# Latent attention in steps of one block of queries, with the projections and the heads' scales cut into pieces between the steps

## The chip, the core and the metric

One core of one Trainium2 chip runs the whole program. The metric is the device time of one execution in microseconds (us). Below, PE is the matrix engine (TensorE), DVE the vector engine (VectorE), ACT the scalar engine (ScalarE), POOL is GpSimd and SP issues the loads. Each engine takes its instructions in one fixed order, which the build of the program sets, and waits at an instruction until what it needs is there.

## What is computed

A trunk of two layers over 512 tokens of width 1,024, in float32. The first layer mixes by a state-space scan and gated linear attention, the second by latent attention with 16 heads; a SwiGLU network follows each. The change is in the latent attention alone:

```python
cq, ckv, k_rope = jnp.split(h @ w_dqkv, [384, 384 + 256], axis=-1)
q = (rms_norm(cq, q_lora_norm) @ w_uq).reshape(bsz, seqlen, H, 64 + 32)
kv = (rms_norm(ckv, kv_lora_norm) @ w_ukv).reshape(bsz, seqlen, H, 64 + 64)
...
q_nope = rms_norm(q_nope, q_nope_norm)
q_rope = apply_rope(rms_norm(q_rope, q_rope_norm), cos[:, None, :], sin[:, None, :])
k_nope = rms_norm(k_nope, k_nope_norm)
...
p = jax.nn.softmax(jnp.where(mask, s, -jnp.inf), axis=-1).astype(v.dtype)
return jnp.einsum('bhqk,bkhv->bqhv', p, v)   # blocks of 128 queries, causal
...
return o @ w_o
```

So each head's queries are scaled twice (64 plain and 32 rotated numbers) and its keys once, by factors that are known only when all of a head's numbers for a token are there.

## The kernel before, in words

Dense products run in three passes of split float32 (`mm3`, L159 to L163): a weight is loaded on SP (`wraw`), split by ACT into `whi` (L155) and by DVE into `wlo` (L156), and multiplied into one of three PSUM accumulators (`acc`, `NACC = 3`), which ACT or DVE empties. There are two more PSUM buffers for scores (`sco`), two for transposes of probabilities (`ptr`), and one for the values' product (`po`).

The attention layer begins with the low-rank products for queries (`q`, three columns) and keys and values (`kv`, two), each followed by the tokens' factors: eight tiny products with ones (L847), then on DVE the mean squares `lm` (L849 to L851), a Newton iteration (`rsqrt`, L176 to L181, tiles `lri`, `lry`, `lrt`) and a last product (L853) into `cf`.

`project(g)` makes one of four groups of four heads: four blocks of queries `qs` (products of 384 columns, emptied by ACT at L911 with the factor of `q`), four blocks of keys and values (512 columns, emptied at L924 and L925 with the factor of `kv`), and then the heads' scales: squares on ACT (L929, L932), their sums on DVE (L930, L931, L933), `rsqrt` over all three kinds at once (`hri`, `hry`, `hrt`), and the scaling and rotation of the whole group (L938 to L945, with `rope` at L863 to L866).

`prepare` transposes the keys (L952) and queries (L965) of a pair of heads on PE and copies them to `kT` (L959 on ACT, L961 on DVE) and `qT` (L967 on ACT). `attend` does a pair: for each of four blocks of queries, the scores of both heads (L984), the negative row minimum on DVE with the mask (L987), the exponential on ACT (L989), the reciprocal (L992) and the scaling (L995) on DVE, transposes on PE (L998), copies to `pt` on ACT (L1002); then the values' product for all blocks (L1007) and its split into `xh`, `xl`. `o_round` is the output projection of four pairs, added to `X` at L1026.

The calls at the end set the order: both first groups are projected, then the pairs follow each other, with the next pair's `prepare` before each `attend`, `project(2)` and `project(3)` behind pairs 0 and 2, and `o_round(0)` behind pair 4. A scheduler of the build moves instructions forward from there by priority, weights by 90 places, so that dense products of a later call fill in between a pair's steps.

```python
pr = {0: project(0), 1: project(1)}
ready = prepare(0, 0, *pr[0])
for p in range(8):
    g, hp = divmod(p, 2)
    cur = ready
    if p < 7:
        ready = prepare((p + 1) // 2, (p + 1) % 2, *pr[(p + 1) // 2])
    attend(g, hp, pr[g][2], *cur)
    if p in PROJ:
        pr[2 + PROJ.index(p)] = project(2 + PROJ.index(p))
    if p == 4:
        o_round(0)
```

Of the kernel before, what the change touches and what calls it, by code (L numbers as in the profile page):

```python
# [18 lines left out]
P = 128  # L19
# [13 lines left out]
PROJ = (0, 2)  # L33
# [16 lines left out]
def kernel(ctx: ExitStack, tc: tile.TileContext, A, yT, stop=99):  # L50
# [120 lines left out]
    def rsqrt(pool, m, shape, tag, ytag=""):  # L171
# [3 lines left out]
        t = pool.tile(shape, F32, tag=tag + "t", name=nm(tag + "t"), bufs=1)  # L175
        V.tensor_scalar(h, m.bitcast(I32), 1, None, ALU.logical_shift_right)  # L176
# [609 lines left out]
    with tc.tile_pool(name="mla", bufs=2) as mp, tc.tile_pool(name="mla1", bufs=1) as m1:  # L786
# [40 lines left out]
        lora, cf = {}, {}  # L827
        for who, n0, n in (("q", 0, 3), ("kv", 3, 2)):
            lora[who], ssq = [], None
            for c in range(n):  # L830
                w = weight(A["w_dqkv"][n0 + c], KD, P)
                ps = acc()
                dense(ps, w, xp)
                hi = m1.tile([P, T], F32R, name=nm("lh"))
                lo = m1.tile([P, T], F32R, name=nm("ll"))
                g = col(who + "_lora", c)
                S.activation(hi, ps, AF.Copy, scale=g)
                V.scalar_tensor_tensor(lo, ps, g, hi.bitcast(F32), ALU.mult, ALU.subtract)
                lora[who].append((hi, lo))
                sq = res.tile([P, T], F32, tag="sq", name=nm("lsq"), bufs=2)  # L840
                S.activation(sq, ps, AF.Square)
                if ssq is not None:
                    V.tensor_tensor(sq, sq, ssq, ALU.add)
                ssq = sq
            ps = aux()
            for i in range(4):
                E.matmul(ps[:, i:i + 1], ssq[:, i * P:(i + 1) * P], ones[:, 0:1], start=True, stop=True)  # L847
# [6 lines left out]
            cf[who] = f  # L854

# [43 lines left out]
        def project(g):  # L899


            qs = mp.tile([P, 4, 4, 96], F32, tag="qs", name=nm("qs"))
            wqs = [weight(A["w_uq"][g, :, k0:k0 + n], n, 384) for k0, n in ((0, 2), (2, 1))]
            for i in range(4):
                ps = acc()
                for k in range(3):
# [4 lines left out]
                S.activation(qs[:, i].rearrange("p h d -> p (h d)"), ps[:, :384], AF.Copy,  # L911
                             scale=cf["q"][:, i:i + 1])
# [3 lines left out]
            v = mp.tile([P, 4, 4, 64], F32, tag="v", name=nm("v"), bufs=3)  # L916
            for i in range(4):
# [16 lines left out]
            for j, n in enumerate((64, 32, 64)):  # L934
                V.tensor_scalar(st[:, j], st[:, j], 1.0 / n, EPS, ALU.mult, ALU.add)
# [81 lines left out]
        def o_round(r, nxt=None):  # L1017

            for m2 in range(4):
                w = weight(A["w_o"][r, m2], 4, 256)  # L1020
                for j in range(2):
# [5 lines left out]
                    if nxt is not None:  # L1027
                        nxt.add(m)
# [102 lines left out]
```

## Time and profile before

| what | value |
|---|---|
| device time, median of 3 runs | 1362.85 us (1362.34 to 1363.99) |
| the profiled execution | 1362.29 us, of which the span from first to last instruction is 1360.1 us |
| busy in the span | PE 1341.3 us (99%), PE's weight loads 1088.2 us (80%), DVE 811.1 us (60%), ACT 567.5 us (42%) |
| TensorE's granted clock | 1.00 of full speed in all 40 slices |
| attention layer | from about 780 us to about 1,002 us of the span |

Products on PE are pipelined: a row's duration covers its way through the array, and the next one starts before it ends. What a product costs in a full stream is the distance from its start to the next start. Busy time therefore hides short waits, and the text below goes by starts. On DVE and ACT, too, an instruction that does not need the one before it starts some 0.07 to 0.1 us before that one's end.

### The profile page before, as it was taken

How to read it: one execution, taken by the hardware profiler on the slowest of the kernel's cores; microseconds unless marked ns; L12 is line 12 of the kernel's file. 1: busy time of each engine (PE TensorE's matmuls, PEld its weight loads, DVE VectorE, ACT ScalarE, POOL GpSimd, SP SyncE). 2: the span in 40 equal slices, each digit the busy share in tenths (PEclk: the TensorE clock that was granted, in tenths of full speed). 3: DMA queues.
4: the chain of work that ended last, by engine and by line, in shares of the span. 5: the costliest groups of instructions: out<-in, count | busy, mean ns of one | idle time of the engine just before them, and what ended most of it. 6: DMA issues, size and time to landing. Idle time of an engine off the chain costs nothing.

```text
span 1360.1 us, 16680 instructions
## 1 busy us (share of the span) xinstructions
PE 1341.3 (99%) x6506; PEld 1088.2 (80%) x6506; DVE 811.1 (60%) x1363; ACT 567.5 (42%) x946; POOL 7.8 (1%) x35
## 2 busy tenths in 40 slices
PE   9999999999999999999999999999999999999998
PEld 5798889888888888888888887657688888888887
DVE  7877977878876444444333569776584444443221
ACT  7575624644353322322222358775653223222121
POOL 0000000000000000000000000000000000000000
PEclk9999999999999999999999999999999999999999
DMA  5342232322232223323333321111033332233331
GB/s 178 123 142 79 78 109 70 95 71 63 90 97 93 93 94 103 98 93 93 98 101 97 102 67 55 32 47 62 4 106 93 94 104 97 93 96 106 112 103 64
DMA packets 36782, 122.23 MB, mean 90 GB/s; under 512 B 4768, under 2 KB 5792, under 8 KB 36704
## 3 DMA queue, kind: packets, MB, share of 16 engines
q1 hardware_dynamic: 35888, 120.72, 28.6%
q8 instruction: 51, 0.84, 0.2%
q10 hardware_dynamic: 816, 0.46, 0.1%
q14 instruction: 27, 0.22, 0.0%
HBM read 119.03 MB, written 2.13 MB: 89 GB/s over the span
## 4 chain that ended last, share of the span: by engine, by line
PE 89%; DVE 7%; ACT 3%; issue 1%; DMA 0%; SPq 0%; DVEq 0%; ACTq 0%
PE acc L161 27%; PE acc L162 27%; PE acc L163 26%; PE sco L984 2%; PE ptr L998 1%; PE po L1007 1%; DVE wlo L156 1%; PE a L496 1%; DVE cva L406 1%; PE a L693 1%; PE a L682 0%; PE a L480 0%; ACT whi L155 0%; PE a L500 0%; PE a L695 0%
## 5 line engine op out<-in xcount | busy, mean ns | idle before, releaser
L155 ACT CAST whi<-wraw 128x1024 fp32r<-128x1024 f32 (+2 forms) x221 | 225.7, 1022 | 548.1 <-PE acc L162 425.0
L161 PE MATMUL acc<-xh,whi 128*128 128x512 f32 x1144 | 449.5, 393 | 2.8 <-ACT qT L967 1.6
L162 PE MATMUL acc<-xl,whi 128*128 128x512 f32 x1144 | 447.5, 391 | 0.0
L163 PE MATMUL acc<-xh,wlo 128*128 128x512 f32 x1144 | 447.2, 391 | 0.0
L156 DVE TENSOR_TENSOR wlo<-wraw,whi 128x1024 fp32r<-128x1024 f32 (+2 forms) x221 | 261.8, 1185 | 159.0 <-ACT whi L155 158.7
L161 PEld LDWEIGHTS acc<-xh,whi 128*128 128x128 f32 x1144 | 214.7, 188 | 47.9 <-ACT qT L967 1.8
L163 PEld LDWEIGHTS acc<-xh,wlo 128*128 128x128 f32 x1144 | 214.8, 188 | 45.2 <-issue 0.7
L162 PEld LDWEIGHTS acc<-xl,whi 128*128 128x128 f32 x1144 | 214.9, 188 | 44.2 <-issue 1.0
L756 DVE TENSOR_TENSOR fu<-acc,R 128x512 f32<-128x512 f32 x44 | 30.4, 691 | 137.1 <-PE acc L163 137.1
L163 PE MATMUL acc<-fhh,wlo 128*128 128x512 f32 x288 | 112.0, 389 | 0.0
L161 PE MATMUL acc<-fhh,whi 128*128 128x512 f32 x288 | 112.0, 389 | 0.0
L162 PE MATMUL acc<-fhl,whi 128*128 128x512 f32 x288 | 112.0, 389 | 0.0
L753 DVE TENSOR_TENSOR fg<-acc,R 128x512 f32<-128x512 f32 x44 | 30.4, 691 | 88.7 <-PE acc L163 88.6
L162 PEld LDWEIGHTS acc<-fhl,whi 128*128 128x128 f32 x288 | 54.1, 188 | 11.3
L161 PEld LDWEIGHTS acc<-fhh,whi 128*128 128x128 f32 x288 | 54.1, 188 | 11.2
L163 PEld LDWEIGHTS acc<-fhh,wlo 128*128 128x128 f32 x288 | 54.1, 188 | 11.1
L162 PE MATMUL acc<-mxl,whi 128*128 128x512 f32 x128 | 50.0, 392 | 0.0
L161 PE MATMUL acc<-mxh,whi 128*128 128x512 f32 x128 | 49.7, 390 | 0.0
L163 PE MATMUL acc<-mxh,wlo 128*128 128x512 f32 x128 | 49.7, 390 | 0.0
L984 PE MATMUL sco<-kT,qT 96*128 96x128 f32 (+3 forms) x128 | 42.8, 445 | 1.5 <-DVE mx L987 1.3
L987 DVE CUSTOM_DVE_ANT_0 sc<-sco,am 128x128 f32<-128x128 f32 (+3 forms) x64 | 30.7, 487 | 13.6 <-PE sco L984 11.5
L989 ACT ACTIVATE sc<-sc,mx 128x128 f32<-128x128 f32 (+3 forms) x64 | 35.7, 561 | 7.3 <-DVE mx L987 7.0
(345 smaller groups left out, 1583.8 us busy)
## 6 DMA issues: line engine op xcount, KB each, us to landing
wraw<-in_w_gate_dram SPq DMA_DIRECT2D x44, 512.0 KB, 3.5
wraw<-in_w_up_dram SPq DMA_DIRECT2D x44, 512.0 KB, 3.5
wraw<-in_w_down_dram SPq DMA_DIRECT2D x32, 512.0 KB, 3.5
wraw<-in_w_out_dram SPq DMA_DIRECT2D x16, 512.0 KB, 3.5
wraw<-in_w_xbc_dram SPq DMA_DIRECT2D x12, 512.0 KB, 3.6
wraw<-in_w_down_dram SPq DMA_DIRECT2D x16, 384.0 KB, 3.1
wraw<-in_w_z_dram SPq DMA_DIRECT2D x8, 512.0 KB, 3.5
wraw<-in_w_v_dram SPq DMA_DIRECT2D x8, 512.0 KB, 3.5
```

Source lines behind the costliest of these rows:

```text
L155: S.copy(hi[:, :kc * m], r)
L156: V.tensor_tensor(lo[:, :kc * m], r, hi.bitcast(F32)[:, :kc * m], ALU.subtract)
L161: E.matmul(out, ah, bh, start=first, stop=False)
L162: E.matmul(out, ah, bl, start=False, stop=False)
L163: return E.matmul(out, al, bh, start=False, stop=last)
L406: V.scalar_tensor_tensor(a, xpad[:, k:k + T], cw[:, 12 * k + i:12 * k + i + 1], a, ALU.mult, ALU.add)
L496: E.matmul(pd[64 * h:64 * h + 64, c * P:(c + 1) * P], xdt[:, c, h, :], mt[:, h, c, :], start=True, stop=True)
L753: V.tensor_tensor(g, pg, R, ALU.mult)
L756: V.tensor_tensor(u, pu, R, ALU.mult)
L984: E.matmul(ps[:, :n], qts[j][:, b * P:(b + 1) * P], kts[j][:, :n], start=True, stop=True)
L987: V.tensor_tensor_reduce(sc[:, :n], ps[:, :n], am[:, T - n:], -scale, 3e38, ALU.add, ALU.min, mx[:, j:j + 1])
L989: S.activation(sc[:, :n], sc[:, :n], AF.Exp, bias=mx[:, j:j + 1], scale=-1.0, accum_out=sm[:, j:j + 1])
```

## The change

- The work of a pair becomes a class with three pieces: `scores(b)`, `transposes(b)` and `values()`. A loop over steps s = 4 p + b gives PE, in each step, the transposes of step s - 1, the scores of step s + 1, and then pieces from a written plan: one block of a projection, a column of `o_round(0)`, or a `prepare`. The values' product of a pair comes in the second step of the next pair. The transposes of both heads wait for the later head's scaling, so that they go in one run; scores are held behind the transposes of the step before.
- `project` is cut into `queries`, `keys` and `heads_norm`. The sums of squares go in pieces of 512 numbers, and scaling and rotation by pairs of heads, instead of for a group at once.
- At the start of the layer: queries of group 0 between the two low-rank products of `kv`; then half of the queries of group 1, the keys of group 0, the rest of group 1's queries and group 1's keys. Group 0's scales come in two Newton iterations, queries first, keys later.
- Copies that empty accumulators get a high priority in the scheduler.

```diff
+        for c in range(3):
+            low_rank("q", 0, c)
+        token_factors("q", 3)
...
+        def sums(g, js):
+            qs, ks, _, st = pr[g]
+            for j in js:
+                x = (qs[:, :, :, 0:64], qs[:, :, :, 64:96], ks)[j]
+                n = (64, 32, 64)[j]
+                x = x.rearrange("p i h d -> p (i h) d")
+                for lo in range(0, 16, T // n):
...
+                    S.activation(sq, x[:, lo:hi], AF.Square, scale=n ** -0.5)
+                    V.tensor_reduce(st[:, j, lo:hi], sq, AX.X, ALU.add)
+                    yield
+        def factors(g, j0, j1, ytag=""):
+            m = pr[g][3][:, j0:j1]
+            V.tensor_scalar(m, m, EPS, None, ALU.add)
+            return rsqrt(mp, m, [P, 3, 16], "hr", ytag, rows=j1 - j0)
+        def apply(g, hp, rq, rk):
+            qs, ks = (t[:, :, 2 * hp:2 * hp + 2] for t in pr[g][:2])
+            V.tensor_tensor(ks, ks, of_pair(rk, hp, 64), ALU.mult)
+            V.tensor_tensor(qs[:, :, :, 0:64], qs[:, :, :, 0:64], of_pair(rq[:, 0], hp, 64), ALU.mult)
+            yield
+            rr = mp.tile([P, 4, 2, 32], F32, tag="rr", name=nm("rr"), bufs=1)
+            V.tensor_tensor(rr, qs[:, :, :, 64:96], of_pair(rq[:, 1], hp, 32), ALU.mult)
+            rope(qs[:, :, :, 64:96], rr, tabs[0], [P, 4, 2, 32])
+            yield
+        def heads_norm(g):
+            yield from sums(g, (0, 1, 2))
+            rf = factors(g, 0, 3)
+            yield
+            for hp in range(2):
+                yield from apply(g, hp, rf, rf[:, 2])
...
+        low_rank("kv", 3, 0)
+        run(queries(0))
+        low_rank("kv", 3, 1)
+        token_factors("kv", 2)
+        run(sums(0, (0, 1)))
+        rq = factors(0, 0, 2)
+        first = queries(1)
+        next(first)
+        next(first)
+        run(keys(0))
+        run(sums(0, (2,)))
+        rk = factors(0, 2, 3, "k")[:, 0]
+        run(apply(0, 0, rq, rk))
+        run(first)
+        mms = list(keys(1))
...
+        put(q2, (0, 0), (0, 1), (0, 2), (0, 3))
+        put(n1, (0, 0), (0, 1), (0, 2), (0, 3), (0, 3), (1, 0), (1, 0), (1, 1), (1, 3), (2, 0))
+        put(k2, (1, 0), (1, 1), (1, 2), (1, 3))
+        put(get_ready(2), (1, 2))
...
+        put(o0, (4, 1), (4, 3), (5, 1), (5, 3), (6, 0), (6, 2), (7, 0), (7, 1))
...
+        for s in range(34):
+            behind = None
+            if s % 4 == 1 and s > 1:
+                pairs[s // 4 - 1].values()
+            if 0 < s < 33:
+                p, b = divmod(s - 1, 4)
+                behind = pairs[p].transposes(b)
+            scores(s + 1, behind)
+            for pieces in plan.get(divmod(s, 4), ()):
+                next(pieces, None)
```

`of_pair` picks the factors of two heads; `low_rank` and `token_factors` are the old loop's body, cut in two.

Three places of the new order. The first is DVE at the factors of `kv` (`lm`, `lri`, `lry`, `lrt`), which the emptying of the keys' accumulators needs. Before:

```order
L849 SCALAR_TENSOR_TENSOR lm_1126_6472<-sco_1125_6467,rtok_1083_6208 128x4
L872 TENSOR_TENSOR krtok_6496<-sco_1130_6491,rtok_1083_6208 128x128
L850 TENSOR_TENSOR lm_1126_6472<-lm_1126_6472,rtok_1083_6208 128x4
L875 TENSOR_TENSOR krsq_6498<-krtok_6496 128x128
L851 TENSOR_SCALAR lm_1126_6472<-lm_1126_6472 128x4
L176 TENSOR_SCALAR lri_1127_6476<-lm_1126_6472 128x4
L177 TENSOR_SCALAR lry_1128_6477<-lri_1127_6476 128x4
```

Now, with the sums of squares of group 0's queries (`st` from `hsq`) and their Newton iteration (`hri`, `hry`) between:

```order
L851 SCALAR_TENSOR_TENSOR lm_1144_6576<-sco_1143_6571,rtok_1083_6208 128x4
L852 TENSOR_TENSOR lm_1144_6576<-lm_1144_6576,rtok_1083_6208 128x4
L954 TENSOR_REDUCE st_1125_6476<-hsq_1148_6595 128x8
L853 TENSOR_SCALAR lm_1144_6576<-lm_1144_6576 128x4
L954 TENSOR_REDUCE st_1125_6476<-hsq_1149_6598 128x8
L177 TENSOR_SCALAR lri_1145_6580<-lm_1144_6576 128x4
L954 TENSOR_REDUCE st_1125_6476<-hsq_1150_6601 128x16
L178 TENSOR_SCALAR lry_1146_6581<-lri_1145_6580 128x4
L960 TENSOR_SCALAR st_1125_6476<-st_1125_6476 128x32
L180 TENSOR_TENSOR lrt_1147_6582<-lry_1146_6581 128x4
L177 TENSOR_SCALAR hri_1151_6605<-st_1125_6476 128x32
L181 SCALAR_TENSOR_TENSOR lrt_1147_6582<-lm_1144_6576,lrt_1147_6582 128x4
```

Three sums and the queries' Newton steps now stand inside the chain of `lm`; on PE only 13 products of the keys of group 0 stand behind the ones products before a fourth accumulator is needed.

The second is PE in the second pair, around the transposes for the pair after it (`acc` from `ks` and `qs`). Before:

```order
L952 MATMUL acc_1306_7224<-ident_105,ks_1177_6734 128x128 x4
L965 MATMUL acc_1307_7231<-ident_105,qs_1163_6671 96x128 x4
L965 MATMUL acc_1309_7238<-ident_105,qs_1163_6671 96x128 x3
L984 MATMUL sco_1281_7138<-kT2_6533,qT_1197_6838 128x256
...
L998 MATMUL ptr_1285_7150<-ident_105,sc_1282_7140 128x128 x2
L998 MATMUL ptr_1286_7155<-ident_105,sc_1284_7145 128x128 x2
L984 MATMUL sco_1297_7186<-kT2_6533,qT_1197_6838 128x512
L161 MATMUL acc_1355_7369<-whi_1350_7359,lh_1089_6286 128x384
```

Now:

```order
L1034 MATMUL sco_1295_7143<-kT2_6434,qT_1242_6955 128x512
L1034 MATMUL sco_1297_7148<-kT3_6436,qT_1244_6962 128x512
L160 MATMUL acc_1299_7156<-whi_1272_7068,lh_1121_6469 128x512
...
L992 MATMUL acc_1300_7165<-ident_105,ks_1185_6757 128x128 x4
L1008 MATMUL acc_1301_7172<-ident_105,qs_1154_6619 96x128 x4
L1008 MATMUL acc_1303_7179<-ident_105,qs_1154_6619 96x128 x4
L1057 MATMUL ptr_1305_7186<-ident_105,sc_1285_7106 128x128 x3
L1057 MATMUL ptr_1306_7191<-ident_105,sc_1287_7111 128x128 x3
L1034 MATMUL sco_1311_7200<-kT0_6430,qT_1302_7177 128x128
```

Before, no dense product stood between the scores and transposes of this pair until its last block; now a block of the keys of group 2 stands behind each block's scores, and the next pair's transposes come before its last-but-one block's own.

The third is DVE where a group's scaling meets the row minima (`sc`, `mx` from `sco`). Before:

```order
L987 ISA sc_1290_7163,mx_1287_7159<-sco_1289_7161,am_6224 128x384
...
L938 TENSOR_TENSOR qs_1237_6958<-qs_1237_6958,hry_1260_7070 128x16x64
L941 TENSOR_TENSOR rr_1262_7084<-qs_1237_6958,hry_1260_7070 128x512
L945 TENSOR_TENSOR ks_1251_7021<-ks_1251_7021,hry_1260_7070 128x1024
L863 TENSOR_TENSOR rt_1263_7086<-rr_1262_7084,csq_6212 128x16x16
L864 TENSOR_TENSOR rt_1263_7086<-rr_1262_7084,csq_6212 128x16x16
L865 TENSOR_TENSOR qs_1237_6958<-rr_1262_7084,csq_6212 128x16x32
L987 ISA sc_1292_7168,mx_1287_7159<-sco_1291_7166,am_6224 128x384
```

Now:

```order
L971 TENSOR_TENSOR ks_1185_6757<-ks_1185_6757,hry_1269_7051 128x4x128
L972 TENSOR_TENSOR qs_1154_6619<-qs_1154_6619,hry_1269_7051 128x4x2x64
L1045 RECIPROCAL sm_1223_6885<-sm_1223_6885 128x2
L1040 ISA sc_1237_6932,mx_1234_6928<-sco_1236_6930,am_6224 128x512
...
L1047 TENSOR_SCALAR sc_1225_6888<-sc_1225_6888,sm_1223_6885 128x384
L1047 TENSOR_SCALAR sc_1227_6893<-sc_1227_6893,sm_1223_6885 128x384
L1040 ISA sc_1239_6937,mx_1234_6928<-sco_1238_6935,am_6224 128x512
```

A block of six instructions for four heads stood between the minima of two heads; now two instructions for two heads stand there, and the rest follows later.

## Rows read from the trace of the kernel before

**Rows 1.** Windows: columns are stretch, its length, busy PE, PEld, DVE, ACT, POOL, clock, DMA share.

```profile
792.00:831.20 39.20, 37.05 (x199) 32.01 (x197) 30.15 (x91) 26.03 (x45) 1.75 (x3) 1.00 0.20 61
831.20:855.00 23.80, 23.00 (x124) 17.44 (x125) 19.99 (x58) 20.77 (x47) 0.00 (x0) 1.00 0.23 77
855.00:985.00 130.00, 122.20 (x630) 82.05 (x629) 90.11 (x274) 85.01 (x219) 0.00 (x0) 1.00 0.10 33
905.00:941.50 36.50, 36.50 (x188) 26.75 (x189) 23.46 (x56) 16.41 (x38) 0.00 (x0) 1.00 0.14 44
941.50:979.70 38.20, 36.81 (x197) 22.61 (x195) 24.16 (x89) 27.09 (x80) 0.00 (x0) 1.00 0.04 15
985.00:1002.00 17.00, 17.00 (x76) 14.07 (x75) 16.16 (x24) 11.20 (x17) 0.00 (x0) 1.00 0.38 112
```

**Rows 2.** Timeline of PE, first and last late start: start us, us, instruction, [idle before].

```profile
804.37 0.34 PE L161 MATMUL acc<-whi,lh 128*128 128x384 f32 x1
804.70 1.02 PE L847 MATMUL sco<-ones,lsq 128*128 128x1 f32 x8
...
977.30 2.38 PE L1007 MATMUL po<-pt,v 128*64 128x512 f32 x16
980.36 0.96 PE L161 MATMUL acc<-xh,whi 128*128 128x512 f32 x3 [0.69 <-ACT xh L137]
```

**Rows 3.** Timeline of PE, end of the start-up, around the first pair's transposes.

```profile
826.29 0.60 PE L952 MATMUL acc<-ident,ks 128*128 128x128 f32 x4
827.44 1.05 PE L965 MATMUL acc<-ident,qs 128*96 128x128 f32 x8 [0.55 <-ACT v L925]
829.46 0.66 PE L952 MATMUL acc<-ident,ks 128*128 128x128 f32 x4 [0.97 <-ACT qT L967]
...
831.35 0.64 PE L965 MATMUL acc<-ident,qs 128*96 128x128 f32 x4 [0.57 <-DVE kT L961]
```

**Rows 4.** Timeline of PE, the longest wait inside the pairs.

```profile
861.90 1.12 PE L984 MATMUL sco<-kT,qT 96*128 96x512 f32 x2
864.37 0.45 PE L161 MATMUL acc<-whi,lh 128*128 128x384 f32 x1 [1.35 <-ACT qT L967]
864.66 0.34 PE L162 MATMUL acc<-wlo,lh 128*128 128x384 f32 x1
864.83 0.34 PE L163 MATMUL acc<-whi,ll 128*128 128x384 f32 x1
```

**Rows 5.** Timeline of DVE, the same stretch.

```profile
861.77 1.22 DVE L938 TENSOR_TENSOR qs<-qs,hry 128x1024 f32<-128x1024 f32 x1
862.90 0.68 DVE L941 TENSOR_TENSOR rr<-qs,hry 128x512 f32<-128x512 f32 x1
863.50 1.22 DVE L945 TENSOR_TENSOR ks<-ks,hry 128x1024 f32<-128x1024 f32 x1
864.64 0.42 DVE L863 TENSOR_TENSOR rt<-rr,csq 128x256 f32<-128x256 f32 x1
864.98 0.42 DVE L864 TENSOR_TENSOR rt<-rr,csq 128x256 f32<-128x256 f32 x1
...
865.91 0.55 DVE L987 CUSTOM_DVE_ANT_0 sc<-sco,am 128x384 f32<-128x384 f32 x1
```

**Rows 6.** Timeline of DVE, the token factors of the queries, first step and eleventh.

```profile
793.24 0.16 DVE L849 SCALAR_TENSOR_TENSOR lm<-sco,rtok 128x4 f32<-128x4 f32 x1 [1.15 <-PE sco L847]
...
795.22 0.16 DVE L181 SCALAR_TENSOR_TENSOR lry<-lrt,lry 128x4 f32<-128x4 f32 x1
```

**Rows 7.** Timeline of ACT, keys and values leave an accumulator.

```profile
810.92 0.45 ACT L924 ACTIVATE ks<-acc,lry 128x256 f32<-128x256 f32 x1
811.27 0.47 ACT L925 ACTIVATE v<-acc,lry 128x256 f32<-128x256 f32 x1
811.63 0.47 ACT L924 ACTIVATE ks<-acc,lry 128x256 f32<-128x256 f32 x1
```

More of the change, by code (lines that the diff above doesn't have):

```diff
@@ L32 @@
 NACC = 3
-PROJ = (0, 2)
 R0F = 7
@@ L950, in prepare @@
+        def heads_norm(g):
+            yield from sums(g, (0, 1, 2))
+            rf = factors(g, 0, 3)
+            yield
+            for hp in range(2):
+                yield from apply(g, hp, rf, rf[:, 2])
+        def prepare(g, hp, behind=None):
+            qs, ks = pr[g][:2]
             ps = acc()
             for i in range(4):
-                E.transpose(ps[:, i * P:(i + 1) * P],
-                            ks[:, i, 2 * hp:2 * hp + 2, :].rearrange("p h d -> p (h d)"), ident)
+                tr = E.transpose(ps[:, i * P:(i + 1) * P],
+                                 ks[:, i, 2 * hp:2 * hp + 2, :].rearrange("p h d -> p (h d)"), ident)
+                if behind is not None:
+                    order(tr, behind, "keys behind products that run until they are normalised")
@@ L983, in attend @@
                     ps = aux("sco")
-                    E.matmul(ps[:, :n], qts[j][:, b * P:(b + 1) * P], kts[j][:, :n], start=True, stop=True)
+                    i = E.matmul(ps[:, :n], self.qts[j][:, b * P:(b + 1) * P], self.kts[j][:, :n],
+                                 start=True, stop=True)
+                    if behind is not None:
+                        order(i, behind, "scores in one go with the transposes of two blocks before")
                     sc = mp.tile([P, T], F32, tag="sc", name=nm("sc"), bufs=SC)
@@ new lines, in run @@
+        def run(pieces):
+            for _ in pieces:
+                pass
+        low_rank("kv", 3, 0)
[13 more added lines that the diff above has]
+        mms = list(keys(1))
@@ new lines, with put, get_ready @@
+        ahead = [None] * 9
+        ahead[0] = prepare(0, 0, mms[1])
+        a0 = apply(0, 1, rq, rk)
+        plan = {}
+        def put(pieces, *places):
+            for place in places:
+                plan.setdefault(place, []).append(pieces)
+        def get_ready(p):
+            ahead[p] = prepare(p // 2, p % 2)
+            yield
+        n1 = heads_norm(1)
+        q2, k2, n2 = queries(2), keys(2), heads_norm(2)
+        q3, k3, n3 = queries(3), keys(3), heads_norm(3)
+        o0 = o_round(0)
```

196 lines of the change are left out of this document (108 added, 88 removed).

## The prediction

> **What bounds the kernel now.** I read the page first: PE is busy 99% of the span, at a granted clock of 1.00 in every slice. Then the windows, since an average says nothing of one layer. Outside the attention layer PE is never free: 76 products of 512 columns in 17.00 us, 0.224 us each, with no idle time [rows 1]. The change does not touch that part, and the order of all instructions before 788 us stays. In the layer PE is idle 2.15 us of 792 to 831.2, 0.80 us up to 855 and 7.80 us of 855 to 985 [rows 1], 10.75 us together. More is hidden, because a pipelined product counts as busy while the next one waits. So I went through PE's timeline from 804 to 985 start to start, against each form's usual distance (0.173 us for 384 columns [rows 4], 0.224 for 512, 0.11 for a transpose). Starts that are 0.15 us or more late number 45 and lose **19.8 us**; the first and the last are in [rows 2]. By stage: 5 of them, 3.1 us, before the first scores at 831.2; 7, 2.2 us, up to 855; 33, 14.5 us, in the remaining pairs. That is the pot: 19.8 us, 1.5% of the time, is all that an order of the same products can win.
>
> What causes them? In the start-up PE comes to the first pair's transposes at 826.29 and waits three times (0.55, 0.97, 0.57 us idle) for accumulators and scaled keys [rows 3]. Inside the pairs the longest wait, 1.35 us at 864.37, ends with a copy of queries on ACT [rows 4], at the moment when DVE runs the scaling of group 2 in one piece: from 861.77 to 865.91 six instructions stand ahead of the next minimum, 4.14 us [rows 5]. PE had nothing else in its order there.
>
> **The change, part by part.** Products, transposes, loads and weight splits are the same in number and size, so PE's work does not change; only late starts do. SP's loads keep their order by group and still come early: PE's waits in the rows are for ACT and DVE, none for a load. That part costs nothing, and its cover is the two weight buffers that ACT and DVE fill ahead.
>
> *Splitting the scales.* By starts, a DVE instruction of 1,024 numbers holds its engine 1.14 us, one of 512 0.60, one of 256 0.34 [rows 5]. Five sums of 512 numbers (3.0 us) replace three (1.14 + 0.60 + 1.14 = 2.9). Scaling and rotating a group took 2 x 1.14 + 3 x 0.60 + 2 x 0.34 = 4.8; it becomes twice 2 x 0.60 + 3 x 0.34 + 2 x 0.15 (the last estimated on the same line), 5.0. Four groups: 1.2 us more on DVE; group 0's second Newton iteration adds 11 steps of 0.20 [rows 6], 2.2 us. Together 3.4 us on an engine that was busy 110 us of the 154 between 831.2 and 985 [rows 1].
> [...]
>
> *The start-up.* Here I expect a loss. The emptying of the keys' accumulators needs the factors of `kv`. Their chain has 15 dependent steps of 0.198 us (793.24 to 795.22 is ten of them [rows 6]), 3.0 us. Now three sums of 0.60 and the queries' Newton steps stand between, so I put it at 3.0 + 1.8 + 0.4 = 5.2 us. Then keys and values leave the first block in 0.72 us [rows 7], with 0.2 for the signals: 6.1 us after the ones products. Behind those, PE has 13 products before it needs that accumulator back (one block in work and two more; there are three accumulators): 13 x 0.23 = 3.0. PE waits **3.1 us**.
> Next, the first pair's keys. Between the factors of `kv` and the scaled keys DVE's order holds: scaling of one pair and rotation of the other (3.7), six sums (3.6), three weight splits (1.14 + 0.87 + 0.47, the last two by the line through the lengths of [rows 5]), the keys' 11 Newton steps (2.2), the scaling itself (0.6), together 12.6, and some 1.2 of waiting for ACT's squares and casts. 5.2 + 12.6 + 1.2 = 19.0 us after the ones products. PE is there after 6.1 + 6 x 0.23 + 18 x 0.173 + 24 x 0.23 = 16.1, with 0.9 for accumulators and weights 17.0. It waits **2.0 us**. The first scores then wait for the copies of queries, which stand on ACT behind the last keys, a cast and a square: **1.0 us**. The rotated shared key and a fourth block of queries behind the emptying of the first `kv` column cost 0.7, smaller pieces 0.5. Sum 7.3 us, against 3.1 now: **4.2 us slower**. From below: if DVE had caught up, the nearest rows are the three waits of [rows 3], 2.1 us. From above: all of DVE's 19 us against PE's work alone without the waits above (13.0 us), 6.0, with 1.0, 0.7, 0.5 and 1.8 for late casts, 10.
>
> *The first pair.* It carries what is left of group 1's factors and scaling, some 8 us of DVE work, beside its own minima. Going through both orders by starts I find three waits: 0.35 for the first probabilities, 0.1, and 1.05 us where an accumulator waits for the keys' copy on DVE. 1.5 us against 2.2 now: **0.7 faster**.
>
> *The other seven pairs.* A step's scores are now followed by a dense block (1.6 us for queries, 1.4 for keys, 2.7 for a column of the output), by the transposes of the block before, and by the next scores, before their own transposes come. That is 4 to 5 us of PE work. What it has to cover is two minima, two exponentials, a reciprocal and two scalings, some 3.3 to 4 us for the largest block. So the wait of [rows 4] has cover in every pair and not only where the scheduler found a block. What a covered pair loses is shown by 905 to 941.5, where dense products stand between the steps: PE is busy all 36.50 us [rows 1]. From above it is what a pair loses now, 14.5 / 7 = 2.1 us. I take 0.6 a pair, near the covered stretch because the new steps are like it, not at zero because DVE is held harder in pairs 2 and 4: 4.2 us against 14.5, **10.3 faster**. Behind the last pair, 4 products of the next accumulators now stand between the values' product and its split, which covers the 0.69 us idle of [rows 2]; that is in the 4.2.
>
> **Sum.** 4.2 - 0.7 - 10.3 = -6.8 us. The profiled execution took 1362.29 us, 0.56 under the median of 1362.85; on the median the forecast is **1356.0 us**. With the bounds (start-up 2.1 to 10, first pair 0.5 to 3, others 0 to 14.5) the extremes are 1345.7 and 1370.6, which need all three at one end.
>
> **Rivals.**
> *DVE becomes the bound (slower).* DVE's work after the first scores is 110 us now and about 111 then; the last two pairs carry some 21 of it (8.1 each for a pair without scales, 24.16 / 3 in 941.5 to 979.7 [rows 1], plus sums into `X` and weights), so the first six hold 90. PE's share of those six pairs is three quarters of 153.8 - 16.7 = 137, thus 103 us. In 831.2 to 855, where scales stood in DVE's path, DVE was busy 84% of the time; in 855 to 985 69% [rows 1]. If the cut pieces hold minima and scalings up so that DVE gets to no more than 75% in six pairs, these take 90 / 0.75 = 120 us, 17 of it waiting, and the sum is 7.3 + 17 + 1 - 19.8 = 5.5 us slower: **1368 us**. The gain is gone below about 79%. For it: each group still needs 10.4 us of DVE. Against it: pieces are at most 0.6 us long, and the plan spreads them over ten places.
> *The start-up costs nothing extra.* If the `kv` chain runs alongside the sums, as small independent steps do, and casts come early, the start-up stays at 3 us: 1362.85 - 4.3 - 6.8 = **1351.7**; with pairs wholly covered too, 1348.
> *The gain is eaten (no change).* The build's scheduler sets the order on DVE and ACT by its own idea of durations, so pieces of the plan need not run where they are written. With a start-up of 9 us and pairs that keep half of what they lose now (7.3), the sum is +5.9 - 0.7 - 7.2 = -2.0: **1361**.
>
> **Chances.** 0.2% of 1362.85 is 2.7 us, about what a measurement of this kernel can tell from no change; so faster means under 1360.1 and slower over 1365.6. The forecast with its near surroundings (1352.5 to 1360): 0.58. Start-up without loss: 0.20. Gain eaten: 0.13. DVE bound: 0.09. Faster is the first two, 0.78. For 8 times in 10 the range leaves out most of the slower case and the deepest gain: 1348.5 to 1362.5.
>
> **What would show it.** Right: between the ones products of `kv` and the first scores PE is idle about 5 us, first at the fourth block of keys of group 0 (released by ACT at the copy of values), then at the first pair's key transposes (released by DVE); from the second pair to the last values' product PE's idle time is below 3 us where it was 7.8; the clock stays at 1.00; the rest of the program takes as long as before. Wrong: if waits for the probabilities' scaling (DVE) before transposes grow in pairs 2 to 5, the rival of DVE holds; if PE does not wait at the fourth block of keys, my 5.2 us chain was too long.

## The result and the profile after

The changed kernel takes **1354.55 us** (median of 4 runs, 1353.58 to 1355.37) against 1362.59 us for the kernel before beside it: ratio 0.9939, 95% interval 0.9922 to 0.9956. That is 8.0 us faster, outside the 0.2% that a measurement can tell; forecast were 1356.0 us and a range of 1348.5 to 1362.5. The profiled execution took 1354.72 us, its span is 1352.5 us, 7.6 less than before. The trace of e1_kv_first below is that of a second execution (e1_again), since its first profile came from a disturbed run.

Three stages, by the starts of the first scores and of the last values' product: first scores at 829.95 us before and 835.48 now; last values' product at 977.30 and 968.30. The start-up is counted from the last product of PE up to which both kernels have the same order. PE's timeline before, that product and the first scores:

```profile
791.17 0.39 PE L162 MATMUL acc<-xl,whi 128*128 128x512 f32 x1
...
829.95 0.39 PE L984 MATMUL sco<-kT,qT 96*128 96x128 f32 x2
```

The same product in the kernel after:

```profile
790.39 0.39 PE L161 MATMUL acc<-xl,whi 128*128 128x512 f32 x1
```

The changed kernel's profile is there 0.78 us earlier, although PE, DVE and ACT have the same order up to 780 us; the difference stands already at 50 us (PE's 201st product starts at 49.88 us before and at 49.07 now), so it is one between two executions and not of the change. From that product to the first scores it is 38.78 us before and 45.09 now. The order of PE has 4 key transposes (0.44 us) fewer ahead of the first scores now, and 11 output products (11 x 0.226 = 2.5 us) more behind the last values' product. Corrected for these, the start-up lost **6.8 us**, the pairs won 147.35 - 132.82 - 2.5 + 0.44 = **12.5 us**, and what follows won 1.1 us, most of it the wait of 0.69 us in [rows 2]: -6.8, and -7.6 with the 0.8 us ahead of the layer.

Windows of the kernel after, which answer to [rows 1] (same columns):

```profile
792.00:835.40 43.40, 38.32 (x181) 32.85 (x180) 32.06 (x109) 26.62 (x50) 2.44 (x3) 0.92 0.21 64
835.40:860.00 24.60, 24.10 (x132) 18.60 (x133) 22.43 (x81) 20.65 (x57) 0.00 (x0) 1.00 0.16 52
860.00:970.40 110.40, 109.58 (x600) 78.64 (x599) 84.69 (x265) 80.03 (x211) 0.00 (x0) 1.00 0.12 39
985.00:1002.00 17.00, 17.00 (x75) 13.77 (x75) 15.26 (x22) 7.44 (x11) 0.00 (x0) 1.00 0.29 93
```

From the first scores to the end of the last values' product PE is idle 1.3 us. Its idle time now lies in the start-up, 5.1 us of it. The waits of PE in the attention layer of the kernel after (engine, tile and line, releaser: us in total, times, longest):

```profile
PE acc L160 <- ACT v L939: 2.5, 1, 2.5
PE acc L992 <- DVE ks L971: 1.7, 1, 1.7
PE sco L1034 <- ACT qT L1011: 0.7, 2, 0.5
PE sco L891 <- DVE kro L872: 0.5, 1, 0.5
PE acc L160 <- ACT qT L1011: 0.4, 1, 0.4
```

All but the last, and the smaller one of the two at L1034, are the start-up's, at the places that the prediction names. On PE's timeline of the kernel after, with the row that answers to the last one of [rows 2]:

```profile
815.70 0.40 PE L162 MATMUL acc<-whi,ll 128*128 128x512 f32 x1
818.63 0.80 PE L160 MATMUL acc<-whi,lh 128*128 128x512 f32 x1 [2.54 <-ACT v L939]
...
831.44 0.40 PE L162 MATMUL acc<-whi,ll 128*128 128x512 f32 x1
833.51 0.63 PE L992 MATMUL acc<-ident,ks 128*128 128x128 f32 x4 [1.67 <-DVE ks L971]
833.97 1.04 PE L1008 MATMUL acc<-ident,qs 128*96 128x128 f32 x8
835.48 0.49 PE L1034 MATMUL sco<-kT,qT 96*128 96x128 f32 x2 [0.47 <-ACT qT L1011]
...
968.30 2.37 PE L1076 MATMUL po<-pt,v 128*64 128x512 f32 x16
970.61 0.50 PE L161 MATMUL acc<-xl,whi 128*128 128x512 f32 x1
```

What nobody foresaw is the row at 818.63: the first product behind the pause takes 0.80 us where 0.40 is usual. Windows of the kernel after around it; the last three numbers of a row are the granted clock, the DMA share and GB/s:

```profile
817.00:818.00 1.00, 0.00 (x0) 0.00 (x0) 0.97 (x8) 0.26 (x1) 0.00 (x0) 1.00 0.00 0
818.00:824.00 6.00, 5.37 (x15) 4.79 (x16) 5.17 (x14) 4.32 (x10) 0.00 (x0) 0.50 0.00 1
824.00:825.00 1.00, 1.00 (x5) 1.00 (x4) 0.62 (x1) 0.53 (x2) 0.00 (x0) 0.59 0.00 0
825.00:826.00 1.00, 1.00 (x8) 1.00 (x7) 0.39 (x1) 0.81 (x3) 0.00 (x0) 1.00 0.38 37
```

PE stood still from 816.09 to 818.63; its granted clock fell to 0.50 at 818.0 and was back at 1.00 at 824.8. From 818.63 to 824.86 it starts 17 products, 6 of 512 columns and 11 of 384. At the distances that this trace has at a clock of 1.00, 0.233 and 0.175 us, these take 3.3 us and not 6.2 (0.43 and 0.32 us apart): the half clock cost PE 2.9 us here.

### The profile page after: what moved, and what is told of

The parts are those of the page before. It is cut to its first block, busy times and chain, and to the rows that moved or that the text cites. A ratio compares the mean times of both kernels' runs of the same rounds, so it can differ in the third digit from the quotient of the medians.

```text
span 1352.5 us, 16703 instructions
## 1 busy us (share of the span) xinstructions
PE 1338.7 (99%) x6506; PEld 1093.7 (81%) x6506; DVE 814.0 (60%) x1403; ACT 565.9 (42%) x958; POOL 8.5 (1%) x35
## 4 chain that ended last, share of the span: by engine, by line
PE 89%; DVE 6%; ACT 3%; issue 1%; DMA 0%; SPq 0%; DVEq 0%; ACTq 0%
PE acc L161 27%; PE acc L160 27%; PE acc L162 27%; PE sco L1034 2%; PE po L1076 1%; PE ptr L1057 1%; DVE wlo L155 1%; PE a L497 1%; DVE cva L407 1%; PE a L694 1%; DVE sc L1040 1%; PE a L683 0%; PE a L481 0%; ACT whi L154 0%; DVE sc L1047 0%
## 5 line engine op out<-in xcount | busy, mean ns | idle before, releaser
L1034 PE MATMUL sco<-kT,qT 96*128 96x128 f32 (+3 forms) x128 | 41.9, 441 | 1.0 <-ACT qT L1011 0.7
L771 DVE TENSOR_TENSOR x<-x,acc 128x512 f32<-128x512 f32 x16 | 11.0, 688 | 42.9 <-PE acc L162 42.9
```

What stands on the lines that cost most here:

```text
L1034: i = E.matmul(ps[:, :n], self.qts[j][:, b * P:(b + 1) * P], self.kts[j][:, :n], start=True, stop=True)
```

## Experiments

Eleven kernels, each timed beside the kernel before. "Start-up" is the distance from the last common product to the first scores in the profiled execution, "pairs" from there to the last values' product; "old pairs" are e8, e10 and e11. The order moves some products between the stages. The pairs of before, e5, e8, e10 and e11 hold the 11 output products (2.5 us) that stand behind them in the others; the start-ups of before, e8, e10 and e11 hold 4 key transposes (0.44 us) more, that of e11 also 8 transposes of queries (0.9 us).

| kernel | median us | ratio to before (95%) | start-up us | pairs us |
|---|---|---|---|---|
| before | 1362.59 | | 38.78 | 147.35 |
| changed | 1354.55 | 0.9939 (0.9922 to 0.9956) | 45.09 | 132.82 |
| e1 factors of `kv` first | 1353.30 | 0.9925 (0.9911 to 0.9939) | 42.79 | 132.57 |
| e2 pause filled | 1353.02 | 0.9922 (0.9908 to 0.9936) | 42.52 | 132.77 |
| e3 old start-up | 1347.93 | 0.9885 (0.9870 to 0.9901) | 37.62 | 132.17 |
| e9 e3, shared key later | 1348.19 | 0.9893 (0.9878 to 0.9908) | 37.43 | 132.37 |
| e4 whole scales | 1354.08 | 0.9926 (0.9913 to 0.9939) | 43.86 | 132.41 |
| e5 one step ahead | 1391.55 | 1.0204 (1.0190 to 1.0219) | 42.59 | 172.01 |
| e6 no priority | 1354.60 | 0.9930 (0.9916 to 0.9944) | 43.41 | 133.26 |
| e7 more DVE work | 1354.18 | 0.9928 (0.9915 to 0.9941) | 43.79 | 132.80 |
| e8 old pairs | 1362.62 | 0.9996 (0.9987 to 1.0005) | 44.33 | 142.16 |
| e10 old pairs, whole scales | 1362.77 | 0.9994 (0.9985 to 1.0003) | 43.13 | 142.42 |
| e11 old pairs, no priority | 1367.23 | 1.0026 (1.0016 to 1.0035) | 44.41 | 146.45 |

### The start-up: e1, e2, e3, e9

**e1_kv_first** takes the sums out of the chain of `kv`.

```diff
-        token_factors("kv", 2)
-        run(sums(0, (0, 1)))
+        done = token_factors("kv", 2)
+        run(sums(0, (0, 1), done))
...
+                    if behind is not None:
+                        order(i, behind, "sums behind the factors of kv")
```

> The changed kernel, with one edge added: the three sums of squares of group 0's queries, and with them their Newton steps, stand on DVE behind the last step of the token factors of kv, not inside that chain. Nothing is added or left out. My theory (the chain of 4.65 us makes PE wait 2.5 us at the fourth block of keys, and the half clock that follows costs 3 us more): the chain takes 3.0 us, the wait falls to 0.8 us or less, the granted clock stays at 1.00, and some of the gain comes back at the first pair's keys, whose scales are then closer; time 1350 to 1352 against 1354.6 of the changed kernel, about 0.992 of the kernel before. Rival (DVE's total work in the start-up is the limit, not its order): the wait at the scaled keys grows from 1.8 us to 5 us or more, and the time stays within 1 us of 1354.6.

DVE's timeline, first in the changed kernel (first and last step of the chain, the first of the three sums, and the keys' scaling that PE waits for):

```profile
813.00 0.16 DVE L851 SCALAR_TENSOR_TENSOR lm<-sco,rtok 128x4 f32<-128x4 f32 x1 [1.21 <-PE sco L849]
...
813.27 0.68 DVE L954 TENSOR_REDUCE st<-hsq 128x8 f32<-128x512 f32 x1
...
817.49 0.15 DVE L855 TENSOR_TENSOR lry<-lry,rtok 128x4 f32<-128x4 f32 x1
...
832.67 1.29 DVE L971 TENSOR_TENSOR ks<-ks,hry 128x512 f32<-128x512 f32 x2
```

Then in e1_again, the chain alone and the keys' scaling:

```profile
814.40 0.16 DVE L851 SCALAR_TENSOR_TENSOR lm<-sco,rtok 128x4 f32<-128x4 f32 x1 [1.21 <-PE sco L849]
...
817.17 0.16 DVE L856 TENSOR_TENSOR lry<-lry,rtok 128x4 f32<-128x4 f32 x1
...
831.62 1.28 DVE L973 TENSOR_TENSOR ks<-ks,hry 128x512 f32<-128x512 f32 x2
```

And e1_again's waits of PE, and a window behind the longer one:

```profile
PE acc L994 <- DVE ks L973: 3.6, 1, 3.6
PE acc L160 <- ACT v L939: 0.8, 1, 0.8
```

```profile
833.50:836.00 2.50, 2.50 (x11) 2.11 (x10) 2.26 (x6) 2.33 (x4) 0.00 (x0) 0.50 0.20 52
```

> The kernel of e1_kv_first once more, for a profile at full clock. It measured 1353.3 us, 1.3 below the changed kernel, where 2.5 to 4.5 were expected. Theory now (DVE's work up to the first pair's scaled keys is the limit behind the removed wait): the wait at the fourth block of keys is below 1 us and the clock stays at 1.00, but the wait at the scaled keys has grown from 1.8 us to about 5 to 6 us. Rival (the wait at the fourth block is still there, or the clock still falls): wait of 2 us or more there, or a clock below 0.9 in one of 816 to 826 us.

The chain falls from 4.6 to 2.9 us (817.17 + 0.16 - 814.40) and the wait behind it from 2.5 to 0.8, as expected. But the wait at the keys' scaling grows from 1.7 to 3.6 us, and now the clock falls behind that pause. The time falls by 1.25 us, which the two intervals don't separate. Counted from the last common product (at 791.63 us in this profile), PE comes to the keys 4.2 us earlier than in the changed kernel, but the scaling starts only 2.3 us earlier, at 40.0 us instead of 42.3. In e2 below, which keeps the sums in the chain but not the drop of the clock, it starts at 39.7. So the chain makes the first wait, and it is not what the start-up costs: with the clock up, DVE's work up to the scaled keys takes as long with the sums inside the chain as behind it. The growth was smaller than the 5 to 6 us of the second expectation because the scaling came earlier too.

**e2_fill** leaves the pause but gives PE something to do in it.

```diff
+                if g == 0 and i == 3:
+                    po = aux("po")
+                    for _ in range(11):
+                        fm = E.matmul(po, fill[:, 0:P], fill, start=True, stop=True)
+                        order(fm, mm, "filling behind three blocks of keys")
```

> The changed kernel, with 11 products of zeros (512 columns, bf16) on PE between the third and the fourth block of group 0's keys, into an idle PSUM buffer: PE works through the 2.5 us in which it waited; the orders of DVE, ACT and SP are the same. It adds work and takes no wait away. Theory (the drop of the granted clock to 0.50 from 818 to 824.7 follows on PE's pause and costs about 3 us): the clock stays at 1.00 and the time falls by 1.5 to 3 us, to 1351.5 to 1353. Rival 1 (the drop has another cause): the clock falls all the same and the time stays at 1354.6 or rises by what the products overrun, below 0.5 us. Rival 2 (the drop costs nothing, since DVE sets when the first pair's keys are scaled): the clock stays up, PE waits 3 us longer at the keys, time 1354.6.

PE's timeline of e2, DVE's at the keys' scaling, and a window behind the filling:

```profile
817.12 2.55 PE L937 MATMUL po<-fill 128*128 128x512 bf16 x11
819.80 0.50 PE L943 MATMUL acc<-whi,lh 128*128 128x512 f32 x1
```

```profile
831.28 1.29 DVE L985 TENSOR_TENSOR ks<-ks,hry 128x512 f32<-128x512 f32 x2
```

```profile
819.80:826.00 6.20, 6.20 (x30) 5.42 (x31) 6.13 (x15) 6.20 (x14) 0.00 (x0) 1.00 0.02 3
```

The order of DVE, ACT and SP is that of the changed kernel. With 11 products more the kernel is 1.5 us faster; its runs (1352.40 to 1353.44) lie below all of the changed kernel's. The clock stays at 1.00; over a whole execution its mean is 1.000 in all four runs, where the changed kernel's four have 0.997 to 1.000. With the pause filled the drop is gone, and with the drop what it cost: counted from the last common product (at 791.57 us here), the first scores come 2.6 us earlier, nearly all of the 2.9 us that PE lost at half clock. PE still waits 1.7 us for the scaled keys, which come 2.6 us earlier too.

**e3_old_start** keeps steps and plan, and takes the start-up in the order of the kernel before.

```diff
-        low_rank("kv", 3, 0)
-        run(queries(0))
-        low_rank("kv", 3, 1)
-        token_factors("kv", 2)
-        run(sums(0, (0, 1)))
-        rq = factors(0, 0, 2)
-        first = queries(1)
-        next(first)
-        next(first)
-        run(keys(0))
-        run(sums(0, (2,)))
-        rk = factors(0, 2, 3, "k")[:, 0]
-        run(apply(0, 0, rq, rk))
-        run(first)
+        low_rank("kv", 3, 0)
+        low_rank("kv", 3, 1)
+        token_factors("kv", 2)
+        run(queries(0))
+        run(keys(0))
+        run(sums(0, (0, 1, 2)))
+        rf = factors(0, 0, 3)
+        run(apply(0, 0, rf, rf[:, 2]))
+        run(queries(1))
```

> The changed kernel with the start-up in the order of the kernel before: both low-rank products of kv, queries and keys of group 0, one Newton iteration for all three kinds of scales, then queries and keys of group 1; first pair's keys behind the sixth of its eight key blocks as now. Steps and plan are as in the changed kernel. Theory (the steps of one block win about 12 us in the pairs and the new start-up gives about 5 back): waits before the first scores 2 to 4 us, no half clock, time 1348 to 1351. Rival 1 (the pairs only gain because the new start-up has part of group 1's scales done early): the first two pairs lose what the start-up gains, 1354 to 1356. Rival 2 (the start-up order helps): slower than 1356.

All waits of PE in e3's attention layer:

```profile
PE sco L891 <- DVE kro L872: 0.5, 1, 0.5
PE sco L1034 <- ACT qT L1011: 0.5, 1, 0.5
PE ptr L1057 <- ACT pt L1066: 0.2, 1, 0.2
```

1347.93 us, at the lower end of the expectation: 6.6 us faster than the changed kernel, 15 faster than before. The start-up is 7.5 us shorter than in the changed kernel, the pairs are 0.65 us shorter. In the old order 14 products of queries and three blocks of keys, 32 products, stand between the ones products of `kv` and the fourth block of keys, where the changed kernel has 13: that covers the chain and the emptying. Behind the last keys 60 products of group 1 (11.8 us, 815.23 to 827.07) run ahead of the first pair's transposes, where the changed kernel has 42: that covers group 0's scales. Both rivals fall: this start-up takes nothing from the pairs, and the new one doesn't help.

**e9_shared_key_late** moves the first of those waits away, in e3's kernel.

```diff
         run(queries(0))
+        ps = aux()
+        for i in range(4):
+            E.transpose(ps[0:32, i * P:(i + 1) * P], kro[:, i, 0, :], ident)
```

> The kernel of e3_old_start (1347.9 us) with the transposes of the rotated shared key behind the queries of group 0 and not ahead of them, since PE waited 0.50 us for them there. Theory: that wait goes and nothing takes its place, 1347.2 to 1347.6. Rival (the pause only moves to a later wait for DVE): 1347.9 or more; the difference is near what the measurement can tell, so the trace decides.

1348.19 us. The wait for `kro` is gone from the list, the start-up is 0.2 us shorter and the pairs are 0.2 us longer; the first scores wait for `qT` as before. A miss: the time that was expected to go does not show.

### The pairs: e5, e8, e4, e10, e6, e11, e7

**e5_one_ahead** brings scores and their transposes one step closer.

```diff
-            scores(s + 1, behind)
+            if s > 0:
+                scores(s, behind)
```

> The changed kernel with scores one step ahead of their transposes and not two: in each step PE does the transposes of the block before, the scores of this block, then the step's pieces, and so only one step's pieces stand between a block's scores and its transposes. Theory (the gain in the pairs comes from how much PE work stands between a block's scores and its transposes, 3.3 to 4 us being needed): one step's pieces of 1.4 to 2.7 us leave 1 to 2 us uncovered in the steps with the larger blocks, 0.5 us in a mean step, 32 steps: 12 to 20 us slower than the changed kernel, 1366 to 1375, that is, the whole gain and more. Rival (the dense piece alone is cover enough, as scheduler and buffers let the next step's work come forward): within 2 us of 1354.6.

PE's largest wait in e5 (the whole layer), its timeline in a step of the last-but-one pair, DVE's in the same step, and a window of all its pairs:

```profile
PE ptr L1057 <- DVE sc L1047: 20.0, 11, 2.8
```

```profile
976.82 1.88 PE L1034 MATMUL sco<-kT,qT 96*128 96x512 f32 x4
981.55 1.94 PE L1057 MATMUL ptr<-ident,sc 128*128 128x128 f32 x8 [2.85 <-DVE sc L1047]
```

```profile
977.88 0.69 DVE L1040 CUSTOM_DVE_ANT_0 sc<-sco,am 128x512 f32<-128x512 f32 x1 [1.89 <-PE sco L1034]
...
980.52 0.88 DVE L1047 TENSOR_SCALAR sc<-sc,sm 128x512 f32<-128x512 f32 x2
```

```profile
833.59:1005.60 172.01, 147.86 (x727) 102.80 (x727) 110.23 (x346) 104.97 (x266) 0.00 (x0) 0.91 0.10 32
```

37 us slower than the changed kernel, nearly twice the upper end expected. The chain is as long as the prediction put it, 3.3 to 4 us: from the first minimum (977.88) to the end of the scaling (980.52 + 0.88) 3.5 us pass. PE's own scores cover the start of it; behind them PE stands idle for 2.85 us. In the last pairs, where the plan has few pieces left, that stands bare. These waits add to 20.0 us, the upper end of what was expected. What the expectation lacked is the clock: its mean is 0.91 in the 172.01 us of the pairs (0.988 in the run), which is 31 us if it is at 0.50 there and at 1.00 elsewhere. With the products evened out the pairs take 36.7 us more than in the changed kernel; PE's idle time there is 24.2 us instead of 1.2, and the other 14 us fit the half clock: at the distances behind the changed kernel's pause, 0.43 us for 512 columns against 0.233, those 31 us lose at most an estimated 14. The direction is the theory's, and the mechanism with it: what counts in the pairs is how much of PE's work stands between a block's scores and its transposes.

**e8_old_pairs** is the other half of e3: the new start-up, and the pairs in the old order.

```diff
+        for p in range(8):
+            pair = Pair(p, *ready)
+            if p < 7:
+                ready = prepare((p + 1) // 2, (p + 1) % 2)
+            for b in range(4):
+                pair.scores(b, None)
+                pair.transposes(b)
+            pair.values()
...
```

> The start-up of the change alone: its order up to the first scores, its pieces, its cut scales and its priorities, but the pairs in the order of the kernel before (group 1's scales ahead of the first pair, each block's transposes right behind its scores, the next pair's preparation ahead of a pair, whole projections behind pairs 0 and 2, the output round behind pair 4, no rule that holds back the transposes of the first head). Theory (the steps win 11 to 15 us in the pairs, the start-up loses 5): late starts in the pairs of 14 to 18 us as before, the half clock behind the fourth block of keys, time 1366 to 1370, slower than both kernels. Rival (cut scales and priorities win a good part of it in the pairs without the steps): 1362 or less.

1362.62 us, 8.1 above the changed kernel: that much is the steps' share. But it is no slower than the kernel before, where 4 to 7 us were expected. Its start-up loses as the changed kernel's does (44.33 us, 5.6 more than before), so its pairs win some 5 us (142.16 against 147.35) without steps. Two parts of the change could do that, the cut scales and the priority of the emptying copies. Each was taken away with the steps (e4, e6) and without (e10, e11).

**e4_whole** and **e10_old_pairs_whole** scale a whole group in one block of six instructions.

```diff
-            for hp in range(2):
-                yield from apply(g, hp, rf, rf[:, 2])
+            q2, k2 = (t.rearrange("p i h d -> p (i h) d") for t in pr[g][:2])
+            V.tensor_tensor(q2[:, :, 0:64], q2[:, :, 0:64],
+                            rf[:, 0].unsqueeze(2).to_broadcast([P, 16, 64]), ALU.mult)
...
```

> The changed kernel with the scales and rotations of groups 1 to 3 again for a whole group in one piece: six DVE instructions, two of them of 1,024 numbers and one of 512, 4 us together, at the place in the plan where the first pair's piece stood; the scaled rotary part is kept in place, to save memory. Steps, sums, start-up as in the changed kernel. Theory (the gain in the pairs is the cover between a block's scores and its transposes, and 4 to 5 us of cover take up a block of 4 us on DVE only in part): one wait of 1 to 2 us in each of three groups, time 1356 to 1360. Rival 1 (cutting the scales is what wins): most of the 12 us in the pairs is lost, 1362 or more. Rival 2 (the cut does nothing, and its extra instructions cost DVE time): 1354.6 or less.

> The kernel of e8_old_pairs (new start-up, pairs in the old order, 1362.6 us) with the scales of groups 1 to 3 for a whole group in one piece, as in e4_whole. e8_old_pairs was expected 4 to 7 us slower than the kernel before and was equal to it, so its pairs win some 4 us without the steps. Theory A (the cut scales win them where pairs have no cover): 2 to 5 us slower than e8_old_pairs, 1365 to 1367. Theory B (the cut wins nothing here either): within 1.5 us of 1362.6.

Neither is slower: pairs of 132.41 us against 132.82 with steps, 142.42 against 142.16 without. The cut of scales and rotations of groups 1 to 3, named in the change's title, is worth nothing that can be measured here; the sums stayed cut in both.

**e6_no_priority** and **e11_old_pairs_no_priority** drop the priority at the five places of the layer.

```diff
-                with tc.high_priority(offset=FREE):
+                if True:
```

> The changed kernel without the high priority of the copies that empty accumulators in the attention layer (queries, keys and values, transposed keys and queries, output columns); the scheduler then places them by their place in the program. Theory (the steps do the work; emptying is a detail): within 2 us of 1354.6. Rival (the priority is what keeps accumulators free, and with it the dense pieces on time): waits for ACT and DVE at accumulators come back in the pairs, 1358 or more.

> The kernel of e8_old_pairs without the high priority of the copies that empty accumulators. Theory A (the cut scales win the 4 us): within 1.5 us of 1362.6. Theory B (the priority wins them, since accumulators come free in time): 2 to 5 us slower, 1365 to 1367. If neither this nor e10_old_pairs_whole is slower, the 4 us lie in what both keep: the order of the start-up, which takes part of the first groups' work out of the pairs, or the buffers.

With steps it is worth nothing (1354.60). Without them it is worth 4.6 us, and the intervals of e8 and e11 lie apart. PE's waits of this kind in the pairs, in e8 and in e11:

```profile
PE acc L160 <- ACT qT L1011: 1.3, 1, 1.3
PE acc L160 <- ACT qT L1011: 3.6, 3, 1.4
```

Then PE's timeline, twice in e11 and once each in e8 and e10:

```profile
869.40 0.45 PE L160 MATMUL acc<-whi,lh 128*128 128x384 f32 x1 [1.44 <-ACT qT L1011]
...
907.82 0.50 PE L160 MATMUL acc<-xh,whi 128*128 128x512 f32 x1 [1.44 <-ACT qT L1011]
```

```profile
904.08 0.50 PE L160 MATMUL acc<-xh,whi 128*128 128x512 f32 x1 [1.35 <-ACT qT L1011]
```

```profile
902.38 0.50 PE L160 MATMUL acc<-xh,whi 128*128 128x512 f32 x1 [1.35 <-ACT qT L1018]
```

This is the 1.35 us wait of [rows 4]: a dense block waits until ACT has copied transposed queries out of an accumulator. These waits make 2.3 us of the difference; the rest lies in shorter ones. With the 8 transposes of queries that stand in its start-up added, e11's pairs take 147.3 us, as long as before: the priority accounts for all that the pairs of e8 and e10 win. Counted with the same products, the pairs win 12.0 us by the steps without the priority (e6), 4.9 by the priority without steps and whole scales (e10) and 12.5 by all together.

**e7_dve_load** puts work on DVE.

```diff
+            if 4 <= s < 32:
+                V.tensor_scalar(slack, slack, 1.0, None, ALU.mult)
```

> The changed kernel with one more DVE instruction in each of the steps 4 to 31 (the second pair to the last): a scaling of 256 numbers in a buffer that nobody else reads, 0.34 us by starts, 28 times, 9.5 us more on DVE. Rival from the prediction (DVE becomes the bound in the pairs): the time rises by 5 to 9.5 us, to 1360 to 1364. Theory (DVE has slack in the pairs, and the cover between scores and transposes takes up a step that is 0.34 us longer): the time rises by less than 2.5 us.

1354.18 us, and pairs of 132.80 us against 132.82: 28 instructions, some 9.5 us of DVE time, cost nothing.

## Why the prediction was right, and where it was not

**The start-up: mechanism right, one thing missing.** The waits came where they were put and in the sizes given: 2.7 us by starts at the fourth block of keys (3.1 predicted; the chain takes 4.6 us, not 5.2), 1.8 at the first pair's keys (2.0), 0.6 at the first scores (1.0), 0.7 at the shared key (0.7), nothing smaller (0.5). Together 5.8 us, less than the 7.3 forecast. The step that failed is "the clock stays at 1.00": behind the first pause it was at 0.50 for 6.8 us, and the start-up lost 6.8 us instead of 4.2. In e2, where the clock stays up, it lost 42.52 - 38.78 + 0.44 = 4.2 us, what was forecast. That it fits so exactly is luck: the waits came out 1.5 us smaller than the sum, and 1.5 us of the loss stands in none of them. A forecast that makes PE wait must price the time behind the wait as well, 2.9 us behind one of 2.5 in the changed kernel's profile. The 0.2 us "for the signals" in the sum stand in no row; the changed kernel's trace shows 0.15 us: ACT begins to empty the accumulator 0.10 us behind the end of the factors (817.64 to 817.74), and PE goes on 0.05 us behind the end of the copy of values (818.58 to 818.63). Two readings of the kernel before were off, without weight in the sum: its first scores start at 829.95 us and not at 831.2, so that the last wait of [rows 3] lies behind them, at the second pair's transposes; and its longest wait inside the pairs is not the one of [rows 4] but this one:

```profile
905.00 0.50 PE L161 MATMUL acc<-xh,whi 128*128 128x512 f32 x1 [1.60 <-ACT qT L967]
```

**The pairs: right sum, wrong pot.** Forecast were 0.7 + 10.3 = 11.0 us, with the cover for the last wait in it; 12.5 came, and 1.1 behind them. By the prediction's own measure it looks different: starts at least 0.15 us late from the first scores to the last values' product fell from 17.8 to 9.7 us, only 8.1. The other 4.4 us are distances that this measure leaves out: delays under 0.15 us lost 6.9 us and now 4.1, and starts that come earlier than the usual distance, at changes from one kind of product to another, gained 4.5 us and now 6.2. So the 19.8 us were not "all that an order of the same products can win", and of the 9.7 that are left most is no wait: PE is idle 1.3 us in these stages. The windows' idle time, 0.82 us of 110.4, is the better witness, and there the forecast of below 3 us holds.

**What covers the wait.** The prediction read [rows 4] and [rows 5] together, as if DVE's block of 4.1 us made the 1.35 us wait. e8, e10 and e4 take that away: whole blocks cost nothing, and the wait of 1.35 us is left both with cut scales (e8) and with whole ones (e10). e11 points to the copy's place on ACT: without the priority waits of this kind grow from 1.3 to 3.6 us, with ACT's copy as the releaser, as the row of before already said. The chain that the steps cover was rightly sized (3.5 us in e5), and two steps' pieces hide it: the waits for the scaling, 20 us in e5, are down to one of 0.1 us in the changed kernel.

**The rivals.** DVE as the bound is refuted by e7. The rival asked whether DVE can be driven to more than 79% in the pairs with scales. The sum of nine windows of the kernel after, 840 to 930 us (the first numbers are the length and PE, PEld and DVE):

```profile
sum 90.00, PE 88.88 PEld 64.72 DVE 79.30 ACT 72.94 POOL 0.00; mean PE 9.88 PEld 7.19 DVE 8.81 ACT 8.10 POOL 0.00
```

It is 88%, and e7 put more on top without loss. "Costs nothing extra" is e3's start-up, not this one's. "The gain is eaten" asked for pairs that keep half of what they lose; PE's idle time there went from 8.3 to 1.3 us. On DVE the cut was to add 3.4 us by the rows. The page of the profile shows DVE's busy time at 814.0 us against 811.1, 2.9 more. By e7, where some 9.5 us more cost nothing, these are hidden.

**Sum.** Start-up +6.8, pairs -12.5, behind them -1.1: -6.8, and -6.8 was forecast. Two errors of 2.6 us, of opposite sign, cancel. That is luck: the first of them is the clock's, whose drop behind this pause lasted 6.8 us, 3.4 us or not at all in the profiles below. The 0.8 us by which the profiles differ ahead of the layer come on top, and the medians differ by 8.0 us.

## What to carry to other kernels

Put independent matrix work between the scores and the transposes of a softmax, enough for the time that PE would stand idle behind the largest block, measured in place (here 2.85 us); then cut scales, priorities and a loaded vector engine no longer mattered here. Test such parts together and apart: the priority was worth 4.6 us alone and nothing beside the steps. Count a stage from an instruction that both orders share: the last common product lies between 790.39 and 792.02 us in these profiles. And check the start of a stage by itself: the version with the old start-up and the new steps (e3, 1347.93 us, ratio 0.9885, 0.9870 to 0.9901) beats both kernels.

## What the runs showed of the hardware

The same pause of 2.5 us at the fourth block of keys stands in eight profiled executions (changed, e4 to e8, e10, e11), and what the granted clock did behind it differs: 6.8 us at 0.50 in one (the changed kernel), 3.4 us in five, and in two (e5, e10) it stayed at 1.00 up to 840 us. Windows behind the pause, in e8 and in e10, whose order up to the first scores is the same on PE, and on DVE but for the tile in which the scaled rotary part is kept:

```profile
820.20:826.00 5.80, 5.73 (x22) 5.40 (x23) 5.18 (x13) 4.69 (x12) 0.00 (x0) 0.71 0.00 1
```

```profile
819.80:826.00 6.20, 6.19 (x30) 5.41 (x31) 6.13 (x17) 6.20 (x14) 0.00 (x0) 1.00 0.01 3
```

The start-up takes 44.33 us in e8 and 43.13 in e10: 1.2 us for 3.4 us at half clock. Between the changed kernel and e2 it is 2.6 us for 6.8. So the price of this pause differed between these executions, from nothing to 2.6 us beside its own length, and one profile shows one throw of it. The pause of 0.7 to 1.8 us at the first pair's keys in the same kernels was followed by no drop, that of 3.6 us in e1_again by 3.4 us at half clock; but so was one of 1.95 us in e5's pairs:

```profile
870.77 0.85 PE L1057 MATMUL ptr<-ident,sc 128*128 128x128 f32 x6 [1.95 <-DVE sc L1047]
```

There the granted clock is 0.50 from 872.0 to 875.4 us. What decides was not tried. The kernel before, too, has executions at a mean granted clock of 1.000 (1362.6 to 1363.1 us beside e1) and at 0.997 (1365.0 and 1365.7 us); where its clock falls, no trace here shows.
